# Conv taps four at a time ahead of each attention step, attention tiles in a list of their own, two-term sums of squares

## The chip, the cores and the metric

The kernel runs on one core of a Trainium2 chip. The metric is the device time of one execution in microseconds (us), as the median of several. The engines are named as in the profile: PE (TensorE matmul), PEld (its weight loads), DVE (VectorE), ACT (ScalarE), POOL (GpSimd) and SP (SyncE, whose queue issues the transfers).

## The reference

Two layers act on 512 latent and 256 context tokens of width 1024. In each layer a modulated norm is followed by one input projection, whose columns go to four mixers; their outputs are joined, projected and added, and a gated feed-forward part follows. Layer 1 is the last, and gives latent tokens only.

```
xn = rms_norm(x, g_norm1[l]) * (1 + scale1) + shift1
p = xn @ w_in[l]
attn = attend(rope(q), concat([kc, k]), concat([vc, v]))   # 4 query heads, 2 key heads, latent + context keys
four = fft2(...).real @ w_f                                # Fourier mixer
conv = silu(layer_norm(depthwise_conv31(glu))) @ w_pw      # 31 taps, 256 channels
pool = means over windows of 2, 4, 8, 16 minus u, @ w_pool
x = x + gate1 * (concat([attn, four, conv, pool]) @ w_o)
xn = rms_norm(x, g2) * (1 + scale2) + shift2
x = x + gate2 * ((silu(a) * g) @ w_out)                    # a, g = split(xn @ w_in_ff)
```

## The kernel before

Activations lie with channels on partitions: `x` is eight tiles of 128 x 768 (columns 0 to 511 latent, LAT; 512 to 767 context, CTX). A product of two 32-bit tiles is made of three matmuls in a faster type, from a rounded part (a name ending in h) and the rest (ending in l): hh, hl and lh. `mm3` issues the three. ACT makes the rounded part, DVE or POOL the rest.

`mix_phase` does the mixers of a layer. It projects q, k and v (`qkv`), the conv branch (`cv`, `cc`), the pool branch (`pp`) and the Fourier branch (`u`). Attention goes over 24 tiles in layer 0 (128 queries of one head each; the last eight are the small context ones) and 16 in layer 1. A tile's step issues `soft` (scores `S`, row maximum `st` on DVE, exponential and scaling `pr` on ACT) and, two steps later, `flip` (transposes `PT`, their copies `pt`, and for each second head the product `pv`). Between the two, `fill` takes pieces of the other branches, by a budget in `PACE`, and `pull(pace.taps)` issues that many conv taps. The convolution of one half of the channels (b = 0 or 1) is a chain of 31 DVE instructions on `run` in PSUM, 128 x 783 elements each in layer 0; of b = 1 the first ten taps are done on ACT and POOL (`side_taps`), and DVE goes on from their sum `ca`. After the last tap `conv_out` transposes (`lnT`), normalizes (`zt`), transposes back (`lnB`) and projects (`pw`). Then come the output projection `wo`, the sums of squares for the second norm, and the feed-forward part `ffn`: in layer 0 by a scheme with seven products (`Operands`, `fast`), each of whose eleven steps ends in the products `fo` that are added to `x`.

`Norm` sums x squared over the channels: tiles k = 0, 2, 4 are added up on POOL in `acc[0]` (in the trace acca or accb), k = 1, 3, 5 on DVE in `acc[1]` (acda, acdb), and the squares of k = 6 and 7 stay apart. `rstd` then multiplies these four terms by a matrix of ones (`ssq`), and ACT and DVE make the factor `R` of it (a square root and RECIPROCAL). Such a product is in 32 bits, and the trace has two records for each. `apply` needs R for the first operands `xnh` and `xnl` of the next product.

What is written in the program is not the order in which an engine gets it: a scheduler puts the instructions of each engine in order before the run, and the engines then follow that order strictly. Tiles come from pools with a fixed number of buffers. `AL` gives 128 x 768 tiles from one pool of 28, among them the operands `xn` and `mx`, the attention tiles `qst` and `qT`, and the operands of the feed-forward part; `W` gives 128 x 1024 tiles from a pool of 14, among them the weights and `pt`. A tile's first write waits until its buffer's last user is done.

Of the kernel before, what the change touches and what calls it, by code (L numbers as in the profile page):

```python
# [19 lines left out]
P = 128  # L20
# [26 lines left out]
PACE = (Pace(12, 6, 3, 2, 4, 3.0, 0.7, 10), Pace(8, 10, 2, 2, 2, 3.0, 0.3, 8))  # L47
# [3 lines left out]
def kernel(ctx: ExitStack, tc: tile.TileContext, xT, ctxT, vec, cst, dft,  # L51
# [7 lines left out]
    alp = ctx.enter_context(tc.tile_pool(name="alp", bufs=28))  # L59
# [17 lines left out]
    def W(name, dt=F32R):  # L77
        return wp.tile([P, 1024], dt, tag="w", name=name)

# [322 lines left out]
    class Norm:  # L402
# [12 lines left out]
        def square(self, k, sl):  # L415
            if k >= self.direct:
                t = U("sq", "t")
                n = sl.stop - sl.start
                act.activation(out=t[:, 0:n], in_=x[k][:, sl], func=AF.Square)
                if self.direct:  # L420
                    self.late.append((sl, t))
                    return
                if k == 0:
                    self.ps[sl.start] = PT("ssq")
                mm(self.ps[sl.start][:, 0:n], ones, t[:, 0:n], start=k == 0, stop=k == KD - 1)
                return
            i = k % 2
            eng = (pool, dve)[i]
            a = self.acc[i][:, sl]
            new = {(i, t) for t in range(sl.start, sl.stop, NC)} - self.seen  # L430
            if new:
                self.seen |= new
                act.activation(out=a, in_=x[k][:, sl], func=AF.Square)
            else:
                t = U("sq", "t")
                act.activation(out=t[:, sl], in_=x[k][:, sl], func=AF.Square)  # L436
                eng.tensor_tensor(out=a, in0=a, in1=t[:, sl], op=ALU.add)  # L437

        def rstd(self, sl):
            n = sl.stop - sl.start  # L440
            if self.direct:
                ps = PF("ssq")
                terms = [a[:, sl] for a in self.acc] + [t[:, 0:n] for z, t in self.late if z == sl]
                self.late = [z for z in self.late if z[0] != sl]
                for i, t in enumerate(terms):
                    mm(ps[:, 0:n], ones, t, start=i == 0, stop=i == len(terms) - 1)
            else:
                ps = self.ps[sl.start]
# [33 lines left out]
    class Acts:  # L482


        def __init__(self, nm, ctx_=True):
            self.lt = [[AL(f"{nm}{i}{k}") for k in range(KD)] for i in "hl"]
# [10 lines left out]
    class Operands:  # L497
# [7 lines left out]
        def tile_(self, nm, k):  # L505
            if (nm, k) not in self.t:
                self.t[nm, k] = AL(f"{nm}{k}")
# [34 lines left out]
        def third(self):  # L542
            n = self.n
            for nm, o in (("t2", n), ("t3", 0)):
                for k in range(4):
# [53 lines left out]
    def mix_phase(l, norm, A, filler):  # L599
# [363 lines left out]
        def make_qT(i):  # L963
            j, o = qpos(i)
            st = AL("qst")
# [7 lines left out]
            qTs[i] = AL("qT")  # L973
            act.copy(out=qTs[i][:, 0:512], in_=ps[:, 0:512])

        class Tile:
# [24 lines left out]
            def flip(self, pt_):  # L1001

                e = self.h % 2
                for j, (c0, n) in enumerate(((0, 2),) if self.nk == 2 else ((0, 4), (4, 2))):
# [3 lines left out]
                    dst = pt_[j][:, 512 * e:512 * e + P * n]  # L1008
# [4 lines left out]
                if not e:  # L1013
                    return
                po = PT("pv")
                for c in range(self.nk):
                    v = vsb[:, P * (self.k0 + c) + 64 * self.kv:P * (self.k0 + c) + 64 * self.kv + 64]
                    for g in range(2):
                        o = 512 * g + P * (c % 4)
                        mm(po[64 * g:64 * g + 64, 0:P], v, pt_[c // 4][:, o:o + P], start=c == 0, stop=c == self.nk - 1,  # L1020
# [88 lines left out]
        pt_ = None  # L1109
        for i in range(len(tiles) + 2):  # L1110
# [4 lines left out]
            if i >= 2:  # L1115
                t = tiles[i - 2]
                if t.h % 2 == 0:
                    pt_ = [W("pt", F32) for _ in range(1 if t.nk == 2 else 2)]
                t.flip(pt_)
# [84 lines left out]
    def ffn(l, norm, first, second, A, filler):  # L1204
# [84 lines left out]
        def fast_steps():  # L1289
            fast_first()  # L1290
            for s in range(1, ns):
# [7 lines left out]
                if fin:  # L1299
                    wl = [need(("fo", l, NF - 2)), need(("fo", l, NF - 1))]  # L1300
                    for sl, st in streams:
                        out_step(s - 1, sl, st, wo, False)
                        out_step(s, sl, st, wl, True)
                        if not last:
                            n1.rstd(sl)
                else:
# [4 lines left out]
                next(filler, None)  # L1311

# [59 lines left out]
        ns = NF // 2  # L1372
        if FAST[l]:
            fast_steps()
# [31 lines left out]
        return n1  # L1406
# [21 lines left out]
    for l in range(DEPTH):  # L1428
        nxt = mix_phase(l, norm, A, mod_pairs(l, 8, 24))
        filler = mod_pairs(1, 0, 8, False) if l == 0 else iter(())  # L1430
        norm, A = ffn(l, *nxt, filler), None
# [82 lines left out]
```

## Time and profile before

| | |
|---|---|
| median of 3 runs | 1476.81 us (1475.5 to 1477.82) |
| profiled execution, its own time | 1474.25 us |
| its span, first to last instruction | 1472.5 us |
| PE busy | 1417.3 us, 96% of the span |
| DVE / ACT / POOL busy | 945.2 / 600.2 / 199.3 us |
| mean granted clock of PE | 0.99 |

In the rows below a time in the trace counts from the span's start. A row of stretches has the stretch, its length, and then for each engine the busy time in it with the number of instructions in brackets, the granted PE clock as a share of full speed, the busy share of the transfer engines and GB/s. A row of the order of time has start, duration, engine, line, operation, written tile <- read tiles, shapes and a count; what stands in square brackets is the idle time before it, and what ended it. A row of waits has the total, the number and the longest, in us.

### The profile page before, as it was taken

The page shows a single profiled execution, that of the slowest core. Times are in us where ns is not written, and L with a number is a line of the kernel's source. Part 1 is how long each engine was busy: PE and PEld are TensorE (multiplying, and loading weights), DVE is VectorE, ACT ScalarE, POOL GpSimd, SP SyncE. Part 2 cuts the span into 40 slices and gives each one's busy share as a digit, 9 for nine tenths or more (in the row PEclk, how much of TensorE's full clock was granted, in tenths as well). Part 3 has the DMA queues.
Part 4 walks back from the last instruction along what each step waited for, and adds up shares of the span by engine and source line. Part 5 has one row for each costly group of instructions (what it writes and reads, how often), then busy time and mean ns, then how long its engine had stood idle before and what let it go on. Part 6 is the DMA issues. An engine that isn't in the chain of part 4 may idle for free.

```text
span 1472.5 us, 20702 instructions
## 1 busy us (share of the span) xinstructions
PE 1417.3 (96%) x8298; PEld 1217.2 (83%) x8298; DVE 945.2 (64%) x1572; ACT 600.2 (41%) x1035; POOL 199.3 (14%) x161
## 2 busy tenths in 40 slices
PE   7999988999999999999999989999899999999998
PEld 4787766998998999999999968776698888888887
DVE  3569577247986778686877777866545545444444
ACT  4457656436533233332332345666544322222220
POOL 2526420420000000000000035430240000000000
PEclk9999989999999999999999999999999999999999
DMA  9525433320323133222322233356442323333231
GB/s 297 164 87 165 157 110 107 109 71 26 104 70 103 54 91 114 87 68 76 115 86 58 92 111 92 117 169 211 127 114 80 108 86 90 111 101 100 89 98 57
DMA packets 192928, 157.35 MB, mean 107 GB/s; under 512 B 6464, under 2 KB 179520, under 8 KB 192832
## 3 DMA queue, kind: packets, MB, share of 16 engines
q1 hardware_dynamic: 192544, 155.34, 34.4%
q8 instruction: 65, 1.06, 0.3%
q10 hardware_dynamic: 288, 0.69, 0.1%
q14 instruction: 31, 0.25, 0.1%
HBM read 151.81 MB, written 4.19 MB: 106 GB/s over the span
## 4 chain that ended last, share of the span: by engine, by line
PE 83%; DVE 7%; ACT 4%; DMA 4%; issue 1%; POOL 1%; SPq 0%; ACTq 0%; DVEq 0%; POOLq 0%
PE ag L161 35%; PE fo L161 20%; PE wo L161 6%; PE qkv L161 4%; PE cv L161 3%; PE agl L161 3%; PE mod L161 3%; DVE run L669 3%; PE u L161 2%; PE ssq L161 1%; PE S L161 1%; DMA wm<-in_w_mod_dram 1%; PE pv L161 1%; PE PT L167 1%; PE cc L161 1%
## 5 line engine op out<-in xcount | busy, mean ns | idle before, releaser
L1362 DVE SCALAR_TENSOR_TENSOR x<-fo,mod,x 128x512 f32<-128x512 f32 (+1 forms) x264 | 170.7, 657 | 81.0 <-PE fo L161 80.5
L161 PE MATMUL fo<-hl,foh 128*128 128x512 f32 (+1 forms) x528 | 187.7, 356 | 0.0
L161 PE MATMUL fo<-hh,fol 128*128 128x512 f32 (+1 forms) x528 | 187.4, 356 | 0.0
L161 PE MATMUL fo<-hh,foh 128*128 128x512 f32 (+1 forms) x528 | 185.5, 358 | 1.9 <-DVE x L1362 1.4
L161 PE MATMUL ag<-t,fs 128*128 128x384 f32 x720 | 136.6, 336 | 0.9 <-DVE hg L1266 0.9
L161 PEld LDWEIGHTS ag<-t,fs 128*128 128x128 f32 x720 | 125.0, 188 | 6.4 <-issue 1.6
L161 PEld LDWEIGHTS fo<-hh,foh 128*128 128x128 f32 x528 | 99.0, 188 | 16.1 <-DVE x L1362 1.8
L161 PEld LDWEIGHTS fo<-hh,fol 128*128 128x128 f32 x528 | 99.2, 188 | 15.1 <-issue 0.2
L161 PEld LDWEIGHTS fo<-hl,foh 128*128 128x128 f32 x528 | 99.2, 188 | 14.7 <-issue 0.7
L182 ACT CAST foh<-fo 128x1024 fp32r<-128x1024 f32 x44 | 46.2, 1050 | 146.0 <-DMA fo<-in_w_ffn_out_dram 146.0
L161 PE MATMUL ag<-b,fa 128*128 128x384 f32 x480 | 92.6, 336 | 1.5 <-DVE ht L1216 1.5
L105 DVE TENSOR_TENSOR fol<-fo,foh 128x1024 fp32r<-128x1024 f32 x44 | 53.8, 1222 | 54.1 <-ACT foh L182 41.9
L669 DVE SCALAR_TENSOR_TENSOR run<-glu,vt,run 128x512 f32<-128x512 f32 (+1 forms) x98 | 87.0, 887 | 1.0
L161 PEld LDWEIGHTS ag<-b,fa 128*128 128x128 f32 x480 | 83.4, 188 | 3.4 <-DVE ht L1216 1.8
L242 ACT CAST fs<-ff 128x512 fp32r<-128x512 f32 x80 | 45.4, 620 | 75.0 <-DVE ff L246 53.0
L437 POOL TENSOR_TENSOR acca<-acca,sq 128x512 f32<-128x512 f32 (+1 forms) x4 | 4.5, 1117 | 523.8 <-ACT sq L436 523.8
L161 PE MATMUL wo<-mxh,wol 128*128 128x384 f32 (+2 forms) x224 | 73.7, 330 | 0.0
L161 PE MATMUL wo<-mxl,woh 128*128 128x384 f32 (+2 forms) x224 | 73.5, 329 | 0.0
L161 PE MATMUL wo<-mxh,woh 128*128 128x384 f32 (+2 forms) x224 | 73.5, 331 | 0.1
L161 PE MATMUL ag<-xfh,fah 128*128 128x512 f32 (+1 forms) x192 | 71.3, 376 | 1.2 <-ACT xfh L465 1.2
L161 PE MATMUL ag<-xfl,fah 128*128 128x512 f32 (+1 forms) x192 | 71.6, 373 | 0.8 <-DVE xfl L466 0.8
L242 ACT CAST fa<-ff 128x512 fp32r<-128x512 f32 x60 | 35.6, 619 | 90.2 <-PE ag L161 51.7
(319 smaller groups left out, 3308.1 us busy)
## 6 DMA issues: line engine op xcount, KB each, us to landing
wm<-in_w_mod_dram SPq DMA_DIRECT2D x64, 512.0 KB, 4.4
fo<-in_w_ffn_out_dram SPq DMA_DIRECT2D x44, 512.0 KB, 3.3
ff<-in_w_ffn_in_dram SPq DMA_DIRECT2D x40, 512.0 KB, 4.7
fa<-in_w_ffn_in_dram SPq DMA_DIRECT2D x24, 512.0 KB, 4.4
fg<-in_w_ffn_in_dram SPq DMA_DIRECT2D x24, 512.0 KB, 3.9
wm<-in_w_mod_dram SPq DMA_DIRECT2D x40, 256.0 KB, 5.3
wo<-in_w_out_dram SPq DMA_DIRECT2D x16, 512.0 KB, 4.8
wm<-in_w_mod_dram SPq DMA_DIRECT2D x16, 384.0 KB, 3.3
```

The source lines that it names most:

```text
L105: eng.tensor_tensor(out=out, in0=full, in1=b32(hi), op=ALU.subtract)
L161: i = last_pe[0] = pe.matmul(*a, **kw)
L167: i = last_pe[0] = pe.transpose(*a)
L182: act.copy(out=hi[:, :n], in_=raw[:, :n])
L242: act.copy(out=hi, in_=full)
L437: eng.tensor_tensor(out=a, in0=a, in1=t[:, sl], op=ALU.add)
L669: yield dve.scalar_tensor_tensor(out=cacc[b][:, :cwid] if j == CONVW - 1 else run, in0=glu[b][:, j:j + cwid], scalar=tap(b, j), in1=cacc[b ...
L1362: dve.scalar_tensor_tensor(out=x[m][:, sl], in0=ps[:, :n], scalar=modT[l][:, 40 + m, st:st + 1], in1=x[m][:, sl], op0=ALU.mult, op1=ALU.add)
```

## The change

`PACE` gives layer 0 four taps for each attention step instead of two; layer 1 keeps two. A new pool of six tiles (`AT`) holds `qst`, `qT` and `pt`, and in the feed-forward part `b21`, two of `t1` and six of `xf`; the pool of `AL` has 22 tiles instead of 28, and `pt` leaves the pool of `W`. For the sums of squares DVE adds acc[0] and the square of k = 6 into acc[1], so that `rstd` has two terms. At the end of layer 0 the first two operand tiles of layer 1 are made for the latent columns before the context columns of the last step, not after it. In `third` the cuts of t2 and t3 alternate.

```diff
-PACE = (Pace(12, 6, 3, 2, 4, 3.0, 0.7, 10), Pace(8, 10, 2, 2, 2, 3.0, 0.3, 8))
+PACE = (Pace(12, 6, 3, 4, 4, 3.0, 0.7, 10), Pace(8, 10, 2, 2, 2, 3.0, 0.3, 8))
...
-    alp = ctx.enter_context(tc.tile_pool(name="alp", bufs=28))
+    alp = ctx.enter_context(tc.tile_pool(name="alp", bufs=22))
+    tp = ctx.enter_context(tc.tile_pool(name="tp", bufs=6))
...
+    def AT(name, dt=F32R):
+        return tp.tile([P, T], dt, tag="at", name=name)
...
                 if self.direct:
-                    self.late.append((sl, t))
+                    if k < KD - 1:
+                        a = self.acc[1][:, sl]
+                        dve.tensor_tensor(out=a, in0=a, in1=self.acc[0][:, sl], op=ALU.add)
+                        dve.tensor_tensor(out=a, in0=a, in1=t[:, 0:n], op=ALU.add)
+                    else:
+                        self.late.append((sl, t))
                     return
...
-                terms = [a[:, sl] for a in self.acc] + [t[:, 0:n] for z, t in self.late if z == sl]
+                terms = [self.acc[1][:, sl]] + [t[:, 0:n] for z, t in self.late if z == sl]
...
-            for nm, o in (("t2", n), ("t3", 0)):
-                for k in range(4):
+            for k in range(4):
+                for nm, o in (("t2", n), ("t3", 0)):
                     self.cut(nm, k, self.f1[k][:, o:o + n])
...
-            st = AL("qst")
+            st = AT("qst")
...
-            qTs[i] = AL("qT")
+            qTs[i] = AT("qT")
...
-            def flip(self, pt_):
+            def flip(self, pair):
...
+                self.pt = AT("pt", F32)
...
                         if not last:
                             n1.rstd(sl)
+                            if st == 0:
+                                for _ in filler:
+                                    pass
+                                nxt = Acts("xn")
+                                for k in range(2):
+                                    n1.apply(l + 1, 0, k, sl, st, nxt)
```

What the scheduler makes of this is read from the order of the instructions, before and after. On DVE in layer 0, before, the 21 taps of b = 1 (`run<-glu,vt`) stand behind the row maxima (`st<-S`) of the sixteenth attention tile, among the copies of the Fourier branch (`g`) and of the pool branch (`mxl<-pm`):

```order
L995 TENSOR_REDUCE st<-S 128x1
L1010 COPY pt<-PT 128x256
L854 SCALAR_TENSOR_TENSOR mxl_951<-pm,vt,mxh_943 128x512
L815 SCALAR_TENSOR_TENSOR py<-ps,cs,ub_936 64x776 x2
L998 RECIPROCAL st<-st 128x1
L669 SCALAR_TENSOR_TENSOR run<-glu_731,vt,ca_640 128x783
L854 SCALAR_TENSOR_TENSOR mxl_951<-pm,vt,mxh_943 128x256
L105 TENSOR_TENSOR pyl<-py,pyh 128x776
L669 SCALAR_TENSOR_TENSOR run<-glu_731,vt,run 128x783 x2
```

With the change the same chain starts six tiles earlier, and runs of one to four taps stand between the row maxima (`mod` is the modulation, a small branch of its own):

```order
L1004 TENSOR_REDUCE st<-S 128x1
L347 TENSOR_REDUCE mod_99<-mods 128x4
L1007 RECIPROCAL st<-st 128x1
L678 SCALAR_TENSOR_TENSOR run<-glu_734,vt,ca_643 128x783
L348 TENSOR_TENSOR mod_99<-mod_99,vt 128x4
L1007 RECIPROCAL st<-st 128x1
L678 SCALAR_TENSOR_TENSOR run<-glu_734,vt,run 128x783
L1019 COPY pt<-PT 128x256
L678 SCALAR_TENSOR_TENSOR run<-glu_734,vt,run 128x783 x3
```

The 21 taps have moved from behind the branch `u` to beside it. On PE at the end of layer 0, before, all products `fo` of the context columns and the sum `ssq` stand ahead of layer 1's first `qkv`:

```order
L161 MATMUL fo<-hh,foh 128x256
L161 MATMUL fo<-hl,foh 128x256
L161 MATMUL fo<-hh,fol 128x256
L161 MATMUL ssq<-acca,ones 128x256
L161 MATMUL ssq<-acda,ones 128x256
L161 MATMUL ssq<-sq,ones 128x256 x2
L167 MATMUL mods<-ident,me 128x128 x2
L161 MATMUL qkv<-wqh,xnh_8268 128x512
L161 MATMUL qkv<-wql,xnh_8268 128x512
```

With the change `qkv` of the first two tiles stands among the last `fo`, ten groups of three ahead of their end:

```order
L165 MATMUL fo<-hl,foh 128x256
L165 MATMUL fo<-hh,fol 128x256
L165 MATMUL qkv<-wqh,xnh_8121 128x512
L165 MATMUL qkv<-wql,xnh_8121 128x512
L165 MATMUL qkv<-wqh,xnh_8121 128x512
L165 MATMUL qkv<-wql,xnh_8121 128x512
L165 MATMUL fo<-hh,foh 128x256
L165 MATMUL fo<-hl,foh 128x256
```

What moved there is 24 matmuls of layer 1, from behind the second `ssq` to ahead of it.

In the tail of layer 1's mixers PE had the projection `pw` of the conv branch right behind the transposes `lnB`:

```order
L167 MATMUL lnB<-ident,zt_10057 128x128 x6
L167 MATMUL lnB<-ident,zt_10058 128x128 x2
L161 MATMUL pw<-csh,smh 128x512 x2
L161 MATMUL pw<-csl,smh 128x512
```

With the change 28 matmuls of the output projection `wo` stand between the two; these are the last of them:

```order
L165 MATMUL wo_10159<-mxh_8792,wol 128x512
L165 MATMUL wo_10159<-mxh_8793,woh 128x512
L165 MATMUL wo_10159<-mxl_8801,woh 128x512
L165 MATMUL wo_10159<-mxh_8793,wol 128x512
L165 MATMUL pw<-csh,smh 128x512 x2
```

What moved is `wo`, from behind `pw` to ahead of it.

## Rows read from the trace of the kernel before

**Rows 1.** The page: busy time by engine, then the chain that ended last.

```profile
PE 1417.3 (96%) x8298; PEld 1217.2 (83%) x8298; DVE 945.2 (64%) x1572; ACT 600.2 (41%) x1035; POOL 199.3 (14%) x161
PE 83%; DVE 7%; ACT 4%; DMA 4%; issue 1%; POOL 1%; SPq 0%; ACTq 0%; DVEq 0%; POOLq 0%
```

**Rows 2.** Stretches: layer 0's mixers (three rows), then layer 1's (two).

```profile
100.00:160.00 60.00, 56.61 (x461) 44.61 (x461) 50.95 (x70) 41.76 (x69) 33.14 (x22) 1.00 0.40 129
160.00:200.00 40.00, 39.29 (x350) 32.53 (x350) 17.37 (x41) 22.24 (x46) 10.61 (x13) 1.00 0.53 165
200.00:262.00 62.00, 49.15 (x355) 36.86 (x355) 49.01 (x103) 38.90 (x92) 2.83 (x1) 0.83 0.30 90
...
1000.00:1060.00 60.00, 57.97 (x486) 42.33 (x484) 38.96 (x94) 35.41 (x68) 9.98 (x4) 1.00 0.65 198
1060.00:1070.00 10.00, 6.42 (x20) 4.58 (x20) 2.85 (x7) 5.01 (x8) 0.00 (x0) 0.66 0.00 0
```

**Rows 3.** Stretches, instructions on the tile run alone (the taps; DVE, clock, DMA).

```profile
100.00:158.00 58.00, 31.98 (x31) 1.00 0.39 123
158.00:205.00 47.00, 0.00 (x0) 1.00 0.50 157
205.00:237.00 32.00, 21.67 (x21) 0.79 0.28 88
```

**Rows 4.** Stretches, all engines, around the 21 taps of b = 1.

```profile
158.00:205.00 47.00, 43.94 (x403) 35.54 (x402) 22.98 (x45) 27.17 (x54) 15.43 (x15) 1.00 0.50 157
205.00:237.00 32.00, 25.40 (x170) 19.47 (x171) 31.44 (x53) 13.73 (x28) 0.00 (x0) 0.79 0.28 88
```

**Rows 5.** Order of time, DVE: row maxima of attention around the taps.

```profile
199.29 0.94 DVE L995 TENSOR_REDUCE st<-S 128x1 f32<-128x768 f32 x1
...
239.13 0.42 DVE L995 TENSOR_REDUCE st<-S 128x1 f32<-128x256 f32 x1 [0.80 <-PE S L161]
```

**Rows 6.** Waits of PE from 196 to 262 us.

```profile
PE pv L161 <- ACT pt L1012: 2.7, 4, 1.1
PE PT L167 <- ACT pr L999: 2.2, 2, 1.6
PE pm L161 <- ACT pyh L818: 2.0, 1, 2.0
PE fp L161 <- DVE g L908: 1.8, 1, 1.8
```

**Rows 7.** Stretches at the end of layer 0, all engines.

```profile
866.00:870.00 4.00, 2.61 (x22) 2.41 (x22) 4.00 (x6) 0.29 (x1) 0.86 (x1) 1.00 0.00 0
870.00:875.00 5.00, 4.48 (x39) 4.28 (x37) 3.08 (x8) 2.36 (x6) 2.40 (x6) 1.00 0.72 211
875.00:880.00 5.00, 1.54 (x4) 1.27 (x5) 4.75 (x6) 3.03 (x7) 4.12 (x8) 0.86 0.36 105
880.00:885.00 5.00, 5.00 (x21) 3.95 (x20) 4.97 (x6) 1.86 (x3) 3.16 (x2) 0.80 0.38 107
```

**Rows 8.** Order of time at the end of layer 0.

```profile
877.74 1.87 DVE L463 SCALAR_TENSOR_TENSOR xt<-x,a,R 128x512 f32<-128x512 f32 x2
878.46 1.12 PE L161 MATMUL ssq<-acca,ones 128*128 128x256 f32 x2 [3.98 <-POOL acca L437]
879.86 3.18 DVE L466 SCALAR_TENSOR_TENSOR xnl<-xt,mod,xnh 128x512 fp32r<-128x512 f32 x2 [0.24 <-ACT xnh L465]
```

**Rows 9.** Order of time, PE: two terms of a sum of squares in layer 0.

```profile
316.72 0.81 PE L161 MATMUL ssq<-accb,ones 128*128 128x384 f32 x2
317.36 0.81 PE L161 MATMUL ssq<-acdb,ones 128*128 128x384 f32 x2
```

**Rows 10.** Order of time: one add on POOL, the same kind of add on DVE twice.

```profile
854.03 1.30 POOL L437 TENSOR_TENSOR acca<-acca,sq 128x512 f32<-128x512 f32 x1 [523.59 <-ACT sq L436]
854.59 1.29 DVE L437 TENSOR_TENSOR acda<-acda,sq 128x512 f32<-128x512 f32 x1
...
857.36 0.68 DVE L437 TENSOR_TENSOR acda<-acda,sq 128x512 f32<-128x512 f32 x1
```

More of the change, by code (lines that the diff above doesn't have):

```diff
@@ L485, in __init__ @@
         def __init__(self, nm, ctx_=True):
-            self.lt = [[AL(f"{nm}{i}{k}") for k in range(KD)] for i in "hl"]
+            self.lt = [[(AT if nm == "xf" and k < 3 else AL)(f"{nm}{i}{k}") for k in range(KD)] for i in "hl"]
         def at(self, i, k, sl):
@@ L506, in tile_ @@
             if (nm, k) not in self.t:
-                self.t[nm, k] = AL(f"{nm}{k}")
+                self.t[nm, k] = (AT if nm == "b21" or nm == "t1" and k > 1 else AL)(f"{nm}{k}")
             return self.t[nm, k]
@@ L999, in soft @@
                 act.activation(out=pr[:, 0:kw], in_=pr[:, 0:kw], func=AF.Copy, scale=st[:, 2:3])
-            def flip(self, pt_):
-                e = self.h % 2
+            def flip(self, pair):
+                self.pt = AT("pt", F32)
                 for j, (c0, n) in enumerate(((0, 2),) if self.nk == 2 else ((0, 4), (4, 2))):
@@ L1007, in flip @@
                         tr(pt[:, P * c:P * c + P], self.pr[:, P * (c0 + c):P * (c0 + c) + P], ident)
-                    dst = pt_[j][:, 512 * e:512 * e + P * n]
+                    dst = self.pt[:, P * c0:P * (c0 + n)]
                     if j:
@@ L1012, in flip @@
                         act.copy(out=dst, in_=pt[:, 0:P * n])
-                if not e:
+                if self.h % 2 == 0:
                     return
@@ L1018, in flip @@
                     for g in range(2):
-                        o = 512 * g + P * (c % 4)
-                        mm(po[64 * g:64 * g + 64, 0:P], v, pt_[c // 4][:, o:o + P], start=c == 0, stop=c == self.nk - 1,
+                        mm(po[64 * g:64 * g + 64, 0:P], v, pair[g].pt[:, P * c:P * c + P], start=c == 0, stop=c == self.nk - 1,
                            tile_position=(0, 64 * g))
@@ L1108, in mix_phase @@
         pull(pace.taps0)
-        pt_ = None
         for i in range(len(tiles) + 2):
@@ L1115, in mix_phase @@
             if i >= 2:
[L1116 to L1119, printed above, removed]
+                tiles[i - 2].flip(tiles[i - 3:i - 1])
             fill(pace.fill * (1 - pace.share))
@@ L1289, in fast_steps @@
         def fast_steps():
+            nxt = None
             fast_first()
@@ L1311, in fast_steps @@
                 next(filler, None)
+            return nxt
         def first_step():
@@ L1372, in ffn @@
         ns = NF // 2
+        nxt = None
         if FAST[l]:
-            fast_steps()
+            nxt = fast_steps()
         else:
@@ L1405, in ffn @@
             pass
-        return n1
+        return n1, nxt
     lo_eng[0] = pool
@@ L1430 @@
         filler = mod_pairs(1, 0, 8, False) if l == 0 else iter(())
-        norm, A = ffn(l, *nxt, filler), None
+        norm, A = ffn(l, *nxt, filler)
 def _constants():
```

## The prediction

> **What bounds the kernel now.** I read the page first. PE is busy 96% of the span and holds 83% of the chain that ended last [rows 1], so the time falls only if PE gets less work, waits less, or loses less to its slow clock. All that the change can win lies in the 55 us in which PE is idle, in the work that PE does at less than full clock, and in PE work that is dropped.
>
> The stretches say where that is. Beside the branch `u`, from 160 to 200 us, PE works 39.29 of 40 us at full clock. In the next 62 us, where the Fourier branch, the last attention tiles and the conv branch finish, it works 49.15 us, at a mean granted clock of 0.83 [rows 2]. Idle there are 62 - 49.15 = 12.9 us. At the lower of its two clocks (1.2 GHz against 2.4) half the busy time is lost, which is (1 - 0.83) x 49.15, about 8 us. So about 21 of the 62 us are lost in this one stretch, more than anywhere else after the start.
>
> The taps are the reason that I see first. DVE does 31 of them from 100 to 158 us, none from 158 to 205, and 21 from 205 to 237, where they take 21.67 of 32 us [rows 3]. DVE is busy 31.44 us of those 32, and 22.98 us of the 47 before [rows 4]: the load is badly spread. Between 199.29 and 239.13 us DVE does no row maximum [rows 5], so PE gets no new attention tile and lives on the Fourier chain, whose every link waits for an ACT or DVE copy. But the list of waits does not name DVE alone: 2.7 + 2.2 + 2.0 us are waits for ACT copies and exponentials, and only the 1.8 us of `fp` waits for a DVE copy [rows 6].
>
> The second place is the end of layer 0. Idle are 1.4 us from 866 to 870, 0.5 to 875 and 3.5 to 880 [rows 7]; the longest single wait is that of `ssq` for the POOL add, 3.98 us [rows 8]. With the slow clock after it, (1 - 0.86) x 1.54 + (1 - 0.80) x 5.00 = 1.2 us, that makes 6.6 us. The third is the tail of layer 1's mixers, 1060 to 1070 us: 3.6 us idle and 0.34 x 6.42 = 2.2 us lost to the clock, 5.8 us [rows 2].
>
> **Taps and attention tiles.** No tap is added or removed. The 21 taps go beside `u`, where DVE has 47 - 22.98 = 24.0 us free [rows 4], and they need 21.67. They just fit, with the row maxima and copies of attention in between. What that costs PE is read from the stretch in which DVE is already loaded so, 100 to 160 us: PE loses 60 - 56.61 = 3.4 us in 60 there, 5.7%, against 1.8% from 160 to 200 [rows 2]. Over 47 us the difference of 3.9% is 1.8 us of cost.
>
> What it gives: without the taps DVE has some 27 us of work left in the 62 us, and the eight small tiles with the context can run among the Fourier products instead of after them. That they have buffers of their own matters here, because the tile list before is shared with the operands. From both sides: if the stretch became as good as 1000 to 1060 us, where attention and the Fourier branch run together and 2.0 of 60 us are lost [rows 2], some 19 us would come back. If only the wait for a DVE copy went, it would be 1.8 us. The waits for ACT (6.9 us) have other causes and can stay, with perhaps half of the slow clock (4 us) behind them: 21 - 6.9 - 4 = 10. I take 11, toward the better end of the middle, as ACT's copies also queue less when the tiles come evenly. Less the 1.8 us this term is **-9**, with ends of 0 and -17.
>
> The transposes `lnT` and `lnB` now stand under `wo`, where PE was already full; they move, and cost no more there than where they left. The larger free part of `W` can bring weights earlier, but no wait of PE in these 62 us names a weight load [rows 6]; I count nothing. The 22 tiles left in `AL` are fewer, but they lose the attention tiles as users; the reordered cuts of t2 and t3 are as many as before and hidden by products that PE has in hand. Both at 0; were that cover gone, a late cut would cost about 0.7 us, as an add of that kind does [rows 10].
>
> **End of layer 0.** The scheduler puts 24 `qkv` matmuls among the last `fo`. For that, DVE does two `xt` (1.87 us) and two `xnl` (3.18 us) [rows 8] earlier, ahead of some of the additions to `x`. Those queue behind them, and PE waits for those additions, having only a few buffers for `fo`; but it now has `qkv` to do meanwhile. DVE is free for 1.9 us from 870 to 875 [rows 7], so at the least those 1.9 us come back; at the most the whole 6.6. I take **-5**, as the moved matmuls are ready when the longest gap opens, and as the gap from 866 to 870, under R's reciprocal, stays.
>
> **Sums of squares.** `rstd` runs six times with four terms, and two go each time. A term of 384 columns costs PE 317.36 - 316.72 = 0.64 us [rows 9]; one of 256 columns, in proportion, 0.43. Twice in layer 0 (384) and twice in layer 1 (256) this stands in full PE work: 2 x 2 x 0.64 + 2 x 2 x 0.43 = **-4.3**. At the end of layer 0 it is part of the 5 us above. On the other side stand twelve adds on DVE, in a row behind the POOL sum. Alone such an add takes 0.68 us at 512 columns, but 1.29 us when it meets the POOL add that started at 854.03 [rows 10]. The adds wait while other work passes on PE, so I leave them out; at the worst one pair late at each of the four places in front of R, at 2 x 0.68 us, eats the 4.3 and 1 more.
>
> The Trainium skill has a rule that speaks against this part: "SBUF — State Buffer", section "Who interferes with whom", says that a DVE instruction with two SBUF inputs contends with a GpSimd instruction that reads SBUF. The doubled add agrees. By that rule every one of the new adds could pay its double price, which only matters where PE waits behind it, as in my worst case.
>
> **Layer 1.** Its taps keep their pace, but `pt` leaves the weights' pool, and the order after it changes: 28 `wo` matmuls stand between `lnB` and `pw`. They cover the wait in the 5.8 us from 1060 to 1070; I take half, **-3**. The price may be the filling matmuls `mod`, which partly move behind attention: if 1000 to 1060 us became like 100 to 160, it would cost (5.7 - 3.4)% x 60 = 1.4 us; if like layer 0's tail (34% lost), 18. The range of this term is -6 to +4, near the first of these.
>
> **Sum.** -9 - 5 - 4.3 - 3 = -21.3 us. The profiled execution took 1474.25 us, 1.75 of them outside its span, and becomes 1453. It is 2.6 us under the median of the runs, so for the median I say **1456**.
>
> **The rivals.** First: the tail's pace is set by ACT, not by the taps. For it speaks that ACT is named in three of four waits [rows 6]; against it, that ACT is busy only 13.73 of 32 us beside the taps [rows 4]. The tail gives 0 and the rest 12: 1465. Second: the tail and layer 1 give all they can, 17 + 6 + 5 + 4.3 = 32: 1445. Third, on the other side: the DVE-bound stretch only moves. From 158 to 205 us DVE would be busy 22.98 + 21.67 = 44.65 of 47 us, nearly as full as from 205 to 237, where PE loses 6.6 us idle and 0.21 x 25.40 = 5.3 to the clock, 37% of the 32 [rows 4]. As runs of taps stand ahead of row maxima, PE's strict order could hold `u` back behind a late attention tile. At 37% it costs 17.4 us in place of today's 3.1: the tail term turns from -9 to +3, and the kernel takes 1468. It is slower than before only if that stretch loses over 26 of its 47 us; at 60%, 28 us, it takes 1479. Against it: from 100 to 160 us DVE is at 85% with the same mixture, and PE loses 5.7%. Fourth: nothing measurable comes of it, if the layer 1 term is +4 or worse and the tail gives nothing: 1474.
>
> **How the numbers follow.** The forecast, 1450 to 1462: 50%. ACT-bound tail, 1462 to 1467: 18%. All recovered, under 1450: 13%. Stretch moved, but faster still, 1467 to 1473: 9%. No difference: 5%. Slower: 5%. A measurement of this kernel tells about 0.2%, 3 us, from no change. So faster is 0.90, same 0.05, slower 0.05. The range 1446 to 1470 leaves out some 8% below and 12% above.
>
> **What would show it.** The taps of b = 1 should lie between about 158 and 200 us; the 62 us before `wo` should shrink by ten, at a mean clock over 0.9, with row maxima throughout. If PE's wait list between 158 and 205 us names `st` or `pr` at more than 5 us, the third rival is at work. At the end of layer 0 the wait of 3.98 us should be gone, and `qkv` should start before the last `fo`. PE should have 24 `ssq` records less (two for each of twelve products), and no long wait for an add in front of R. From 1060 to 1070 us `wo` should fill what was idle. The forecast is wrong if the first `wo` of layer 0 starts later than about 256 us, if waits for ACT in the tail grow past 10 us, or if PE idles longer than before in layer 1's mixers.

## The result, and the profile after

The changed kernel takes 1452.47 us (median of 4 runs, 1452.05 to 1454.16); the kernel before took 1476.15 us beside it (4 runs, 1474.13 to 1477.82). The ratio is 0.9845, with a 95% interval of 0.9832 to 0.9857: faster by some 23 us, where 21 were forecast. The profiled execution took 1454.16 us, its span is 1452.4.

The page, which answers to [rows 1]: busy time by engine, then the chain that ended last.

```profile
PE 1404.9 (97%) x8274; PEld 1210.4 (83%) x8274; DVE 954.3 (66%) x1584; ACT 598.4 (41%) x1034; POOL 201.5 (14%) x161
PE 82%; DVE 9%; ACT 3%; DMA 3%; POOL 1%; issue 1%; SPq 0%; DVEq 0%; ACTq 0%; POOLq 0%
```

PE has 24 records less, two for each of the twelve products dropped, and DVE has 12 adds more, as counted. Of the 20.1 us by which the span fell, 12.4 are PE work that no longer stands there or runs at the higher clock (1417.3 to 1404.9), and the rest is idle time.

Where it came from is read by five stages, cut at PE's products in the order of time: to the first `ag` of layer 0 (the mixers, with the first sum of squares), to its last `ag`, to the last `cv` of layer 1 (the end of layer 0), to the first `ag` of layer 1, and to the last `fo`. A boundary is the start of the first or the last row of these products in the order of time. The table has their lengths in us, from the traces of the kernel before, of the changed one, and of six of the experiments.

| kernel | mixers 0 | feed-forward 0 | end of 0 | mixers 1 | feed-forward 1 |
|---|---|---|---|---|---|
| before | 336.31 | 508.29 | 87.78 | 168.45 | 367.33 |
| changed | 324.80 | 504.86 | 87.09 | 164.15 | 367.15 |
| two taps | 329.42 | 504.88 | 87.23 | 165.03 | 366.62 |
| no early operands | 326.54 | 504.88 | 91.22 | 166.03 | 367.17 |
| four taps alone | 343.30 | 508.75 | 87.68 | 169.21 | 366.97 |
| list alone | 333.62 | 507.11 | 87.77 | 167.44 | 367.47 |
| list and taps | 323.88 | 507.17 | 87.66 | 166.30 | 367.46 |
| context sum on DVE | 323.18 | 504.85 | 85.95 | 164.65 | 367.15 |

The changed kernel gains 11.5 + 3.4 + 0.7 + 4.3 + 0.2 = 20.1 us. The end of layer 0, for which 5 us were forecast, gives almost nothing. Each row of the table is a single execution. Kernels that differ from the changed one only at the end of layer 0 (no early operands, context sum on DVE) have 323.18 to 326.54 us in the first stage, so a difference of under some 3 us says little there.

In the mixers of layer 0 the stretches of [rows 3] and [rows 4] now read so. The taps alone:

```profile
158.00:205.00 47.00, 22.81 (x21) 1.00 0.46 149
205.00:237.00 32.00, 0.00 (x0) 0.95 0.54 165
```

All engines in the same stretches, and in the 25 us after them:

```profile
158.00:205.00 47.00, 43.64 (x409) 36.17 (x407) 41.61 (x67) 27.52 (x57) 16.89 (x16) 1.00 0.46 149
205.00:237.00 32.00, 31.38 (x264) 25.66 (x264) 15.81 (x46) 21.75 (x60) 0.00 (x0) 0.95 0.54 165
237.00:262.00 25.00, 17.96 (x109) 13.60 (x108) 12.42 (x32) 16.26 (x28) 8.77 (x4) 1.00 0.25 69
```

All 21 taps of b = 1 lie between 158 and 205 us. DVE is busy 41.61 of those 47 us instead of 22.98, and PE loses only 0.3 us by it (43.64 against 43.94). From 205 to 237 us PE works 31.38 of 32 us at a clock of 0.95, where it had 25.40 at 0.79. The row maxima of the context tiles, the first of which stood at 239.13 us in [rows 5], now run from 210.88 to 227 us:

```profile
210.88 0.41 DVE L1004 TENSOR_REDUCE st<-S 128x1 f32<-128x256 f32 x1
...
226.78 0.41 DVE L1004 TENSOR_REDUCE st<-S 128x1 f32<-128x256 f32 x1
```

Then comes what is new: from 237 to 262 us PE is idle for 7 us. Attention is over by 233.4 us, the first `wo` stands at 233.6 instead of 262.3, and PE runs into the conv branch's chain of normalizing copies and into weights that are not there yet. Two rows of the order of time show the latter: PE's wait of 1.67 us for the rounded part of a weight, and the queue of SP, on which four `wo` loads take 26.85 us to be issued. Its longest waits there are for PE's `mod` (9.4 us) and `pw` (8.9 us):

```profile
239.49 0.44 PE L165 MATMUL wo<-mxh,woh 128*128 128x384 f32 x1 [1.67 <-ACT woh L186]
...
234.62 26.85 SPq L192 DMA_DIRECT2D wo<-in_w_out_dram  x4
```

So of the 28.7 us by which `wo` starts earlier, 11.5 arrive at the feed-forward part.

The stretches at the end of layer 0, which answer to [rows 7]:

```profile
860.00:865.00 5.00, 5.00 (x31) 4.31 (x29) 1.30 (x3) 2.30 (x6) 3.42 (x3) 1.00 0.12 36
865.00:870.00 5.00, 0.97 (x3) 0.84 (x3) 3.21 (x4) 2.12 (x5) 3.31 (x7) 0.69 0.68 200
870.00:875.00 5.00, 5.00 (x16) 3.92 (x15) 3.31 (x5) 2.43 (x4) 2.04 (x1) 0.63 0.05 14
```

The order of time there on POOL, DVE and PE, which answers to [rows 8]:

```profile
864.62 2.51 POOL L109 TENSOR_TENSOR wcl<-wc,wch 128x1024 fp32r<-128x1024 f32 x1
865.45 1.96 DVE L446 TENSOR_TENSOR acda<-acda,sq 128x256 f32<-128x256 f32 x1
867.24 0.76 POOL L446 TENSOR_TENSOR acca<-acca,sq 128x256 f32<-128x256 f32 x1
868.03 0.42 DVE L427 TENSOR_TENSOR acda<-acda,acca 128x256 f32<-128x256 f32 x1 [0.62 <-POOL acca L446]
868.56 0.42 DVE L428 TENSOR_TENSOR acda<-acda,sq 128x256 f32<-128x256 f32 x1
869.04 1.22 PE L165 MATMUL ssq<-acda,ones 128*128 128x256 f32 x2 [4.03 <-DVE acda L428]
```

The early `qkv` fill PE to 865 us, and then it waits for `ssq` as long as before, 4.03 us against 3.98. The wait now ends behind two DVE adds in a row, which stand behind a POOL add, which stands behind the split of a weight. The clock falls further after the gap, to 0.69 and 0.63 in the two stretches here, where it was 0.86 and 0.80 in [rows 7]. Counted as the prediction counts, (1 - 0.69) x 0.97 + (1 - 0.63) x 5.00 = 2.2 us of PE's work are lost to it instead of 1.2.

### The profile page after: what moved, and what is told of

Its sections match the earlier page's. It is cut to its first block, busy times and chain, and to the rows that moved or that the text cites. A ratio compares the mean times of both kernels' runs of the same rounds, so it can differ in the third digit from the quotient of the medians.

```text
span 1452.4 us, 20661 instructions
## 1 busy us (share of the span) xinstructions
PE 1404.9 (97%) x8274; PEld 1210.4 (83%) x8274; DVE 954.3 (66%) x1584; ACT 598.4 (41%) x1034; POOL 201.5 (14%) x161
## 4 chain that ended last, share of the span: by engine, by line
PE 82%; DVE 9%; ACT 3%; DMA 3%; POOL 1%; issue 1%; SPq 0%; DVEq 0%; ACTq 0%; POOLq 0%
PE ag L165 35%; PE fo L165 20%; PE wo L165 6%; PE qkv L165 3%; PE mod L165 3%; PE agl L165 3%; PE u L165 2%; PE cv L165 2%; PE pv L165 1%; PE ssq L165 1%; PE S L165 1%; DVE run L678 1%; DMA wo<-in_w_out_dram 1%; PE PT L171 1%; DMA wm<-in_w_mod_dram 1%
## 5 line engine op out<-in xcount | busy, mean ns | idle before, releaser
L186 ACT CAST foh<-fo 128x1024 fp32r<-128x1024 f32 x44 | 46.2, 1050 | 144.0 <-DMA fo<-in_w_ffn_out_dram 142.1
```

Of the source, the lines that this page charges most:

```text
L186: act.copy(out=hi[:, :n], in_=raw[:, :n])
```

## Experiments

Each kernel was timed in five rounds beside the kernel before; differences are given by the ratios, times 1476 us.

**Two taps.** The pace of before in the changed kernel:

```diff
-PACE = (Pace(12, 6, 3, 4, 4, 3.0, 0.7, 10), ...
+PACE = (Pace(12, 6, 3, 2, 4, 3.0, 0.7, 10), ...
```

> The changed kernel with two taps ahead of each attention step of layer 0 again; all else as changed. Theory (the taps set the tail of layer 0): the 21 taps of b = 1 go back behind 200 us, the first wo of layer 0, at 233.6 us in the changed kernel and 262.3 before, comes after 245, and the feed-forward part starts about 10 us later: 1461 to 1464 us. Rival (the attention tiles' own list gives the gain, the taps only follow): the first wo stays before 240 us and the time within 3 us of the changed kernel's 1452.5.

It took 1459.13 us, a ratio of 0.988 (0.9868 to 0.9893), 5 us more than the changed kernel, half of what the theory asked. The first `wo` came at 246.1 us, 12.5 later, but the feed-forward part only 4.6 later (table): what the taps bring forward partly waits again for weights and the conv branch.

**One list.** The attention tiles, and the operands that went with them, back in one list of 28:

```diff
-    alp = ctx.enter_context(tc.tile_pool(name="alp", bufs=22))
-    tp = ctx.enter_context(tc.tile_pool(name="tp", bufs=6))
+    alp = ctx.enter_context(tc.tile_pool(name="alp", bufs=28))
...
     def AT(name, dt=F32R):
-        return tp.tile([P, T], dt, tag="at", name=name)
+        return alp.tile([P, T], dt, tag="al", name=name)
```

> The changed kernel with the attention tiles qst, qT and pt, and the few operands that went with them, back in the one list of 28; four taps, all else as changed. Theory (the taps set the tail): the feed-forward part of layer 0 starts within 3 us of the changed kernel's, 1452 to 1456 us. Rival (the list of their own is what counts): qst, qT and pt wait for operands again, PE's attention tiles come late, the feed-forward part starts about 10 us later, 1461 to 1464 us. A third way: both are needed, then this run and the one with two taps both lose about 10 us.

It took 1488.71 us, 1.0083 (1.007 to 1.0095): 35 us more than the changed kernel and 12 more than before. This was outside of what any of the three ways gave. In its profiled execution 21.8 us of it lie in the mixers of layer 0 (346.55 us) and 13.3 in those of layer 1 (177.45 us), where the taps keep their pace of two. So the loss isn't that of the taps alone; `pt` stands among the operands in no other kernel here, and that this is what layer 1 loses by wasn't tried by itself. The list is not a detail beside the taps; whether four taps do harm without it is asked next, of the kernel before.

**Four taps alone, list alone, list and taps.** The first is the kernel before with a pace of four:

```diff
-PACE = (Pace(12, 6, 3, 2, 4, 3.0, 0.7, 10), ...
+PACE = (Pace(12, 6, 3, 4, 4, 3.0, 0.7, 10), ...
```

The second is the changed kernel with three diffs of this section at once, two taps, four terms and no early operands (the last two stand further down), so that the list, the place of `pt` and the order of the cuts are left. The third is the second with four taps.

> The kernel before with four taps ahead of each attention step of layer 0, and nothing else. The run with one list said that with four taps the shared list loses more than the taps win, but there pt too had gone into that list; here pt stays among the weights. Theory 1 (the taps set the tail by themselves): the feed-forward part of layer 0 starts about 5 us earlier than in the kernel before, 1468 to 1472 us. Theory 2 (four taps need the tiles' own list, since a tile that waits for a buffer stops PE while DVE is full): no gain or a loss, 1475 to 1490 us, with waits of PE in the tail that name PT, pt or qT.

> The kernel before with the attention tiles in a list of their own (pt written by head, six buffers) and the cuts in the other order; two taps, four terms, no early operands. From the run with two taps, the feed-forward part of layer 0 should start 3 to 5 us earlier than before, and the stretch from the last cv of layer 1 to its feed-forward part, 168.5 us before and 164.2 in the changed kernel, should take 165 to 167: theory, 1467 to 1471 us. Rival (the list gives nothing by itself): 1474 to 1478 us.

> The changed kernel with four-term sums and no early operands: the taps and the list together. Theory (the parts add up): the tail gives 10 and layer 1 some 2.5 us, 1461 to 1465 us. Rival (the sums and the early operands give little together, since the runs without each show a part that depends on the other): 1454 to 1459 us. At the end of layer 0 it should stand as the kernel before does, 87 to 88.5 us from the last ag to the last cv.

Four taps alone: 1481.99 us, 1.0048 (1.0036 to 1.0061), 7 us slower than before. List alone: 1469.5 us, 0.9957 (0.9945 to 0.997), 6 us faster. Both: 1461.85 us, 0.9906 (0.989 to 0.9922), 14 us faster, where the two by themselves would add up to nothing. The views by tile show what differs: for each kernel the last query tiles (`qst`, DVE) and the products `pv` (PE) from 195 us on, with count, durations, and the first and last start. The kernel before:

```profile
L969 DVE TENSOR_TENSOR qst<-q,qst x2: 416/417/418, 234.2 to 236.6; 128x256 fp32r<-128x256 f32 x2
L161 PE MATMUL pv<-pt,vsb x104: 272/273/476, 200.6 to 262.1; 128*64 128x128 f32 x104
```

Four taps alone:

```profile
L969 DVE TENSOR_TENSOR qst<-q,qst x2: 415/416/416, 232.7 to 258.2; 128x256 fp32r<-128x256 f32 x2
L161 PE MATMUL pv<-pt,vsb x104: 272/273/477, 200.3 to 272.0; 128*64 128x128 f32 x104
```

The changed kernel:

```profile
L978 DVE TENSOR_TENSOR qst<-q,qst x2: 411/414/416, 206.0 to 219.2; 128x256 fp32r<-128x256 f32 x2
L165 PE MATMUL pv<-pt,vsb x102: 272/273/473, 194.8 to 233.4; 128*64 128x128 f32 x102
```

The two `qst` are the queries of the eight context tiles. In the old lists they are not made before 232 us, with two taps or with four; four taps push the second to 258 us, and the last `pv` to 272. With the list of their own they are made at 206 and 219 us, and the last tiles run beside the Fourier products. The stretch from 210 to 230 us has PE busy 14.70 of 20 us at 0.83 with four taps alone, and all 20 at 1.00 with list and taps:

```profile
210.00:230.00 20.00, 14.70 (x99) 11.36 (x99) 7.37 (x20) 8.04 (x17) 0.00 (x0) 0.83 0.17 53
```

```profile
210.00:230.00 20.00, 20.00 (x175) 16.25 (x173) 10.26 (x34) 15.66 (x48) 0.00 (x0) 1.00 0.51 159
```

DVE is busy only 7.37 of those 20 us with four taps alone. The taps are out of the way there, and PE still waits. The waits that theory 2 asked for are not in the list, though: from 205 to 272 us the longest are 2.7 us for `mxl` and 1.7 for `pyl`, and `pt` and `pr` together make 3.2 (`PT`, `pv` and `S`). The loss shows in the order of the work and not in a wait that names a tile of the list. (The profiled execution of list and taps was 3.3 us faster than that kernel's median.)

**Which tiles of the list.** List and taps once more, first with `pt` written by pairs into the weights' tiles as before (so the list is left to the queries and operands), then with `qst` and `qT` back in the operands' list, now of 22:

```diff
...
-                tiles[i - 2].flip(tiles[i - 3:i - 1])
+                t = tiles[i - 2]
+                if t.h % 2 == 0:
+                    pt_ = [W("pt", F32) for _ in range(1 if t.nk == 2 else 2)]
+                t.flip(pt_)
```

```diff
-            st = AT("qst")
+            st = AL("qst")
...
-            qTs[i] = AT("qT")
+            qTs[i] = AL("qT")
```

> The kernel with the list and four taps alone (four-term sums, no early operands), and with pt written by pairs into the weights' tiles again, as in the kernel before: the list of their own is then left to qst and qT and the few operands. Theory 1 (what counts is that the queries of the last tiles need not wait for the operands' buffers): it stays with the list and four taps, 1459 to 1464 us, and the last pv comes before 240 us. Theory 2 (what counts is pt, out of the weights' tiles): it falls back toward four taps alone, 1472 to 1482 us, and the last pv comes after 250 us.

> The counterpart: the list and four taps alone, with qst and qT back in the operands' list (of 22), and pt in the list of its own. Theory 1 (the queries' buffers): the last two qst come after 225 us instead of 203 and 219, the last pv after 255 us, 1472 to 1485 us. Theory 2 (pt): 1459 to 1464 us.

Neither theory alone: 1479.36 us, 1.0024 (1.0013 to 1.0034), and 1479.79 us, 1.0029 (1.0018 to 1.004). Each half undone costs the 14 us and some 4 more. With the queries in the operands' list the last `pv` is later than in any other kernel, and the second `qst` later than in any but the one with one list (271.8 us):

```profile
L973 DVE TENSOR_TENSOR qst<-q,qst x2: 415/416/416, 230.7 to 259.3; 128x256 fp32r<-128x256 f32 x2
L165 PE MATMUL pv<-pt,vsb x104: 272/273/477, 195.9 to 289.9; 128*64 128x128 f32 x104
```

With `pt` among the weights `qst` still comes at 229.2 us, 12 us later than with list and taps, and the last `pv` at 258.8. So both halves of the list are needed for the gain. That the queries need buffers which operands don't hold, and `pt` buffers which weights don't hold, is the likely reason, but these two runs don't show it alone: with `pt` its packing by pairs came back, and the queries went into a list of 22, where the kernel before had 28. Which tile stood in front of which isn't seen in a trace, since the scheduler settles it in the order before the run.

**Six taps.**

```diff
-PACE = (Pace(12, 6, 3, 4, 4, 3.0, 0.7, 10), ...
+PACE = (Pace(12, 6, 3, 6, 4, 3.0, 0.7, 10), ...
```

> The changed kernel with six taps ahead of each step of layer 0 instead of four. Theory (after 233 us the tail is bound by the weights of wo and by the conv branch's chain, not by the taps): no gain, and as the row maxima stand behind longer runs of taps, PE waits for st between 150 and 200 us: 1453 to 1458 us. Rival (the taps still hold the tail up, so more of them ahead go on giving): 1446 to 1450 us. The third rival of the prediction at its strongest: PE loses over 10 us between 150 and 205 us, and the time is over 1462 us.

1465.59 us, 0.9934 (0.9921 to 0.9947): 13 us more than the changed kernel, more than my theory gave, and the third rival's place isn't where it is lost. Two stretches of six taps:

```profile
150.00:205.00 55.00, 52.34 (x490) 42.84 (x484) 46.68 (x79) 33.37 (x67) 19.79 (x17) 1.00 0.53 168
...
220.00:240.00 20.00, 12.13 (x59) 8.12 (x60) 5.49 (x15) 18.25 (x34) 0.00 (x0) 0.58 0.33 109
```

From 150 to 205 us PE loses 2.7 of 55 us; the changed kernel loses 4.1 there (50.88 busy). From 220 to 240 us PE is busy 12.13 us at 0.58 and ACT 18.25 of 20, against 17.91 at 1.00 and 12.04 in the changed kernel. The taps end earlier, the conv branch's transposes `lnT` move from 237 to 209 us, and their copies on ACT now stand among the last attention tiles: `pv` waits 5.8 us for ACT's `pt`, three times, up to 3.1 us:

```profile
PE pv L165 <- ACT pt L1021: 5.8, 3, 3.1
```

Four taps are a balance of two chains, not a step toward ever more.

**Four terms, and no early operands.** The changed kernel with the old sums of squares, and the changed kernel without the early operands:

```diff
-                    if k < KD - 1:
-                        a = self.acc[1][:, sl]
-                        dve.tensor_tensor(out=a, in0=a, in1=self.acc[0][:, sl], op=ALU.add)
-                        dve.tensor_tensor(out=a, in0=a, in1=t[:, 0:n], op=ALU.add)
-                    else:
-                        self.late.append((sl, t))
+                    self.late.append((sl, t))
...
-                terms = [self.acc[1][:, sl]] + [t[:, 0:n] for z, t in self.late if z == sl]
+                terms = [a[:, sl] for a in self.acc] + [t[:, 0:n] for z, t in self.late if z == sl]
```

```diff
-                            if st == 0:
-                                for _ in filler:
-                                    pass
-                                nxt = Acts("xn")
-                                for k in range(2):
-                                    n1.apply(l + 1, 0, k, sl, st, nxt)
```

> The changed kernel with four terms in every sum of squares again, so without the two DVE adds in front of each. Theory (PE's work is saved, the adds are hidden, and at the end of layer 0 the two adds and the two terms are worth the same 1 us): 4.3 us more, 1456 to 1458 us. Rival 1 (the adds stand in front of R and eat what is saved): 1452 to 1453.5 us. Rival 2 (the adds cost the end of layer 0 its whole gain): without them the wait of 4.0 us in front of ssq there falls under 2 us, and the time is 1453 to 1455 us.

> The changed kernel without the early operands of layer 1, so that the 24 qkv stand behind the second sum of squares as before. Theory of the prediction (they are worth 5 us): 1457 to 1458 us. Rival (they only moved ahead of a wait that stays, since what ends it is the chain of the last squares, POOL add and two DVE adds): 1451 to 1454 us, with the wait in front of ssq still 3 to 5 us, and no more PE idle time from 850 us to the first cv than the changed kernel has, within 1 us.

Four terms: 1460.69 us, 0.9896 (0.9878 to 0.9914), 7.5 us more than the changed kernel. (Its profiled execution took 1468.48 us, the five others 1458.24 to 1461.70, so of its trace only waits are used.) No early operands: 1460.15 us, 0.9884 (0.987 to 0.9898), 6 us more, and the end of layer 0 takes 91.22 us instead of 87.09. That is the prediction's side, against what I had read out of the changed kernel's trace; but both theories missed how. Without the early operands PE's long wait there is another one:

```profile
867.28 0.80 PE L165 MATMUL qkv<-wqh,xnh 128*128 128x512 f32 x1 [6.77 <-ACT xnh L474]
```

The rows of DVE ahead of it say what `xnh` waits for. The `xt` for it stands behind the adds of the context sum, and the two of these take 2.92 us:

```profile
862.30 2.92 DVE L446 TENSOR_TENSOR acda<-acda,sq 128x256 f32<-128x256 f32 x2 [1.26 <-ACT sq L445]
865.15 1.21 DVE L472 SCALAR_TENSOR_TENSOR xt<-x,a,R 128x512 f32<-128x512 f32 x1
866.28 0.41 DVE L427 TENSOR_TENSOR acda<-acda,acca 128x256 f32<-128x256 f32 x1
866.61 0.74 DVE L472 SCALAR_TENSOR_TENSOR xt<-x,a,R 128x512 f32<-128x512 f32 x1
867.28 2.59 DVE L428 TENSOR_TENSOR acda<-acda,sq 128x256 f32<-128x256 f32 x1
```

So the two edits meet at this place. Two-term sums without early operands cost 91.22 - 87.66 = 3.6 us there (list and taps has neither), and the early operands give 4.1 us back. The 3.6 us are the adds together with the order that the scheduler makes of them: here four `qkv` stand ahead of `ssq` on PE, and with list and taps `ssq` stands first. With four terms the early operands bring only 1.5 us over list and taps (0.9896 against 0.9906, within their intervals): the wait for `ssq` is 0.2 us in that trace, but `qkv` waits 2.3 us for `xnh` instead.

**What holds the 4 us in front of ssq.** Two tries: the context sum's adds of tiles 2 and 4 on DVE, so that none waits on POOL behind a split; and the splits of layer 1's first weights on DVE, so that POOL is free.

```diff
...
-            eng = (pool, dve)[i]
+            eng = (pool, dve)[i if not (self.nm == "a" and sl.start >= CTX.start) else 1]
```

```diff
-        lo_eng[0] = pool
+        lo_eng[0] = dve if l else pool
...
         ahead[0] = 2
+        lo_eng[0] = pool
         rope_tables(l)
```

> The changed kernel with the squares of the context columns at the end of layer 0 added up on DVE alone (tiles 2 and 4 too), so that no add of that sum stands on POOL behind the split of a weight (2.51 us). Theory (the POOL queue makes the 4.0 us in front of ssq): the wait falls to 1 to 2 us, the stretch from the last ag to the last cv from 87.1 to about 85, and the time is 1449 to 1451 us. Rival (what counts is that the last square, its DVE add and the two adds stand in a row): the wait stays over 3 us and the time within 1 us of 1452.5. The doubled DVE work there may also delay x and R for the latent columns; then the time is over 1453.

> The changed kernel with the low parts of layer 1's first weights (wq and the first wc) made on DVE, not on POOL; PE's order stays nearly the same. With the context sum on DVE the wait in front of ssq stayed at 3.8 us, and one DVE add there took 1.97 us, as long as a POOL split of 2.46 us beside it was still running; in the changed kernel it is 1.96 us beside one of 2.51 us. Theory (the POOL splits hold DVE's adds and the POOL add up): every add of that chain takes 0.4 to 0.5 us, the wait falls to 1 to 2.5 us, the stretch from the last ag to the last cv from 87.1 to 84.5 to 86, and the time is 1449.5 to 1452 us. Rival (the chain is as long without POOL, because DVE now does the splits itself, about 1.1 us each, in front of the adds): the wait stays over 3 us, the stretch at 86.5 or more, the time 1452 to 1455 us.

Context sum on DVE: 1454.7 us, 0.9868 (0.9853 to 0.9883). Splits on DVE: 1453.47 us, 0.9848 (0.9834 to 0.9861). Neither beats the changed kernel; their end of layer 0 takes 85.95 and 86.19 us instead of 87.09, too little for these intervals. The waits stayed at 3.8 and 3.3 us, so both rivals were nearer than the theories. The rows of the splits on DVE show what is left when no split runs on POOL:

```profile
865.29 0.48 DVE L1375 SCALAR_TENSOR_TENSOR x<-fo,mod,x 128x256 f32<-128x256 f32 x1
865.68 0.55 DVE L446 TENSOR_TENSOR acda<-acda,sq 128x256 f32<-128x256 f32 x1
866.34 0.42 DVE L427 TENSOR_TENSOR acda<-acda,acca 128x256 f32<-128x256 f32 x1
867.22 0.42 DVE L428 TENSOR_TENSOR acda<-acda,sq 128x256 f32<-128x256 f32 x1 [0.46 <-DVE acda L427]
867.70 1.22 PE L165 MATMUL ssq<-acda,ones 128*128 128x256 f32 x2 [3.27 <-DVE acda L428]
```

The slow add of 1.96 us is gone (0.55), and still 2.4 us pass from the start of the last addition to `x` to `ssq`: four DVE instructions in a row, with one split of 1.22 us on DVE just ahead of them. The last `fo` has been done for 3.3 us by then.

## Why the prediction was right, and where not

**Taps and attention tiles.** Forecast 9 us; the stage gained 11.5, of which one sum of squares is 1.3, so 10.2. Read as the term was, from 200 to 262 us: before, 12.9 us idle and 8 lost to the clock; after, PE is busy 30.11 of 34 us at 0.95 and 20.96 of 28 at 1.00, so 10.9 idle and 1.5 lost. That is 8.5 us less, mostly clock. Such figures are of one execution each: list and taps, which has no two-term sums, needs 323.88 us for this stage and so a little less than the changed kernel's 324.80, and they are good to some 3 us. The size was right, the reason only half. I put the taps first and gave the buffers one sentence; the runs show that the taps alone cost 7 us, the list alone gives 6, and both give 14. And "no wait of PE in these 62 us names a weight load; I count nothing" for `pt` leaving `W` was the wrong step: put back, it costs all the gain. The list of waits did not tell this beforehand; the order there may have had these tiles late already, which no run shows. A reading was wrong too: that only 1.8 us of these waits are for DVE holds for the four rows of [rows 6] alone. The list goes on with 1.1 us for `mxl`, 0.9 for `g` and 0.5 for `pt`, all of DVE, so DVE ends 4.3 us.

**The price at the stretch beside u.** 1.8 us forecast, 0.3 measured. PE's waits named neither `st` nor `pr` there; the only one from 158 to 205 us was 3.3 us for a copy `pt` of DVE, behind the pool branch's `py`:

```profile
PE PT L171 <- DVE pt L1019: 3.3, 1, 3.3
```

The third rival was wrong even with six taps.

**The tests.** Taps between 158 and 200 us: yes, 163.7 to 193.4. First `wo` before 256: yes, 233.6. ACT waits in the tail under 10 us: yes. Row maxima throughout: from 210.88 to 227 us, yes, where there were none before 239.13. PE idles less in layer 1's mixers, 9.9 us instead of 13.9. That `wo` would fill 1060 to 1070 us: PE is busy there all of 10 us, but so early only since all is shifted; where `wo` now stands, from 1020 to 1050, 3 us are idle, of which 1.3 are a wait for a weight. The wait of 3.98 us gone, and no long wait for an add in front of R: no, it is 4.03 us.

**End of layer 0.** Forecast 5, measured 0.7. Two steps failed. "The moved matmuls are ready when the longest gap opens": they are ready before it and PE has done them by 865 us; they fill the gaps between the `fo` and leave the last one, with a slower clock after it. And "the adds wait while other work passes on PE, so I leave them out": at this place nothing passes, and the four adds in front of the two R queue with the operands, 3.6 us without the early operands. I had named that price (2 x 0.68 us at each place) and the contention with POOL, but put it into the range and not into the sum. The 0.7 us are less than the four products dropped there are worth alone (4 x 0.43 = 1.7 us): PE's busy time in this stage falls from 81.9 to 80.4 us, and its idle time rises from 5.9 to 6.7.

**Sums of squares.** Forecast 4.3 outside that boundary. The feed-forward stage of layer 0 has 507.1 to 507.2 us in the two kernels with the new list and four terms, and 504.9 in those with two: 2.3 us for one product pair of 1.28. PE's busy time there falls by 0.9 us; the rest is a wait: with four terms PE waits 1.5 us for DVE's `ht` behind the second R, and with two terms not. From 508.29 to 507.15 us a wait for `hg` goes (0.9 us) and one for `hs` comes (0.4 us), and PE's busy time falls by 0.7 us. Two edits of that stage are left for this, the reordered cuts of `third` and the operands in the new list. With the operands in one list and all else as changed the stage takes 505.55 us, so the list is worth 0.7 us of it; no run had the cuts alone. In layer 1 only the first sum stands ahead of the first `ag`, 2 x 0.43 us; the second lies in the last stage, which gained 0.2 us. With 1.28 for the first sum of layer 0 the sums make about 4.7 us.

**Layer 1.** Forecast 3, measured 4.3, of which 0.9 is a sum of squares: 3.4. List and taps has 2.15 of it (168.45 to 166.30). The step held: the two waits of PE in the old tail, here from 1000 to 1075 us of the kernel before, are gone, and with the changed kernel a smaller one for a weight is the longest in the same stretch:

```profile
PE lnB L167 <- DVE zt L1048: 2.2, 1, 2.2
PE pw L161 <- ACT csh L1063: 1.9, 1, 1.9
```

```profile
PE wo L165 <- POOL wol L109: 1.3, 1, 1.3
```

So the sum of 21.3 stands against 20.1 in the profiled executions. The end of layer 0 was put 4.3 too high; the tail gave 1.2 more, the sums 0.4, layer 1 0.4, and the feed-forward stage of layer 0 another 1.1 that the prediction had put at nothing. That most of this cancels is luck, and the forecast owes its near hit in part to it. The fourth rival's own terms, 0 - 5 - 4.3 + 4, make 1471.5 us and not 1474.

The Trainium skill, "SBUF — State Buffer", section "Who interferes with whom", says that a DVE instruction with two SBUF inputs contends with a GpSimd instruction that reads SBUF; this was weighed as what speaks against the new adds. The trace agrees at the place where it matters: an add of 256 columns took 1.96 us beside a POOL split of 2.51 us and 0.55 us with the split moved to DVE. The wait in front of `ssq` is not this contention alone: with the splits off POOL 3.3 of its 4.0 us stayed, with a split of 1.22 us then on DVE itself.

## What to carry to other kernels

When work of one engine is moved, look at which tiles share a buffer list with what it moves beside: a tile that comes late because of its list can show as an order and not as a wait, and a run with a list of its own tells whether the list matters. Two edits that are each worth little or harmful can be worth much together, so undo them one by one and also do them one by one. And matmuls moved ahead of a wait take nothing off it if PE has done them before it starts; then the chain that ends the wait must get shorter.

## What the runs showed of the hardware

The same tap, with both tensor inputs in SBUF, took 1.02 us with POOL idle in the kernel before and 2.20 us while a POOL series ran until 165.04 us in the changed one. These are the rows, first before, then after with the POOL row:

```profile
205.31 1.02 DVE L669 SCALAR_TENSOR_TENSOR run<-glu,vt,ca 128x783 f32<-128x783 f32 x1
```

```profile
163.68 2.20 DVE L678 SCALAR_TENSOR_TENSOR run<-glu,vt,ca 128x783 f32<-128x783 f32 x1
160.01 5.03 POOL L810 TENSOR_TENSOR ps<-ps 128x789 f32<-128x789 f32 x3
```

The next tap takes 1.01 us; its running sum is in PSUM. Such a tap doesn't show the effect: in the kernel before one took 1.03 us at 148.02 us, while a POOL add ran from 147.63 to 149.84 us. It goes the other way too: a POOL split that takes 2.4 us elsewhere took 8.08 us at 878.30 us in the changed kernel, where DVE made operands `xt` and `xnl` without a pause from 875.6 to 884 us:

```profile
878.30 8.08 POOL L109 TENSOR_TENSOR wcl<-wc,wch 128x1024 fp32r<-128x1024 f32 x1 [6.26 <-PE qkv L165]
```
